# Two pairs of value groups merged into token-major groups of 1024 features, the linear attention's heads stepped evenly, the silu groups ended without a flush

## The chip, the core and the metric

The kernel runs on one core of a Trainium2 chip. The time is device microseconds of one execution. Matrix multiplications run on PE (TensorE), elementwise work on DVE (VectorE) and ACT (ScalarE); POOL (GpSimd) and SP (SyncE) here mostly issue transfers (DMAs). "mm" and "sm" are PSUM banks that PE writes, "u" and "ur" are buffers of 128x512 numbers in SBUF.

## The reference

One layer of a decoder trunk, 512 tokens of 1024 features in fp32. Of it, what the change touches:

```python
h = rmsnorm(x, ln1[i])
hq, hk, hv, hr, ha, hatt, hgate = _split_cols(h @ w_in[i], SPLIT_SIZES)
log_a = jax.nn.log_sigmoid((ha @ w_a2[i] + b_a[i]).astype(jnp.float32)) / GLA_TAU
o = gla_mixer(hq..., hk..., hv..., log_a...)              # 4 heads, dk 128, dv 256, chunks of 64 tokens
o = o * lax.rsqrt(jnp.mean(o * o, axis=-1, keepdims=True) + EPS)
o = o.reshape(B, S, GLA_V_W) * gla_gn[i] * jax.nn.silu(hr)
y_gla = o @ w_o_gla[i]
for g, (win, dil) in enumerate(((128, 1), (512, 4), (2048, 16))):
    o_g, lse_g = dilated_attention(q_g, k_g, v_g, bias_g, dil, win // dil)   # 4 heads of 128 each
wts = jax.nn.softmax(jnp.stack(lses, axis=0), axis=0)
o_att = jnp.sum(wts[..., None] * jnp.stack(outs, axis=0), axis=0)
y_att = o_att @ w_o_attn[i]
mix = (jax.nn.sigmoid(g_gla) * y_gla + jax.nn.sigmoid(g_att) * y_att) @ w_out[i]
```

Then an MLP of 4096, an embedding gate and a last norm, which the change leaves alone.

## The kernel before

Every fp32 product is emulated with three matmuls: each operand is split into a high part (`hi` for weights) and a low part (`lo`), and hi·hi, hi·lo and lo·hi are summed in PSUM. The input projection `h @ w_in` is cut into groups of 512 columns: the attention's q, k, v of its three groups (v1, v2 are the values of the two dilated ones, v0 those of the first), then gq, gk, gv0, gv1 of the linear attention (GLA), its output gate r0, r1, and the merge gates gb, ga. Most groups go through `strassen` (L301): a Strassen-Winograd scheme, in which seven products of half-size blocks take the place of eight. Each product is a stage (`STAGES`: A11, S1, A22, S2, A12, S4, S3), named after its weight block; S1 to S4 are sums of blocks A11 to A22. A stage is 24 matmuls of 128x256, all from one weight operand of 128x1024. A finished bank is evacuated by `begin` (to a buffer) or `end`, which adds it and calls the group's `finish`. Value groups are token-major: the tokens are the stationary side, the weights (`hi`, `lo`) stream.

The engines run in the order in which the program issues. `fetch` (L232) makes the weight operands, always at the same lead: in the turn of operand i it writes lo(i) on DVE (L239), hi(i+1) on ACT (L244), the sums S2 and S4 of operand i+2 on DVE (L218, L224), and prepares i+3: a load on SP's queue (L201), and for S1 and S3 an accumulating DMA on POOL's queue (L210, L221), which adds a second block from DRAM to the first. `EARLY` sets the lead of the load for S1: five operands before the group's A11. There are six buffers for loaded blocks, five for hi and four for lo, so that lo(i) waits until PE has used lo(i-4).

Other work runs between the matmuls. `run` (L255) issues pieces of eight matmuls and calls `step` (L179), which executes one entry of the list `later` (evacuations and what follows them) and, each `pace` streamed columns, one part of a generator in the list `side`. A yield is the end of a part. The generators are the scores and softmax of the attention (`scores0`, `scores12`), `weights` (the merge of the groups' softmax statistics), `pv`, `decay`, `gla(h)` (one head of the linear attention) and `gla_out`. `drain` issues whatever is left in both lists, `flush` whatever is left in `later`.

Three places matter below. `scores12` writes the softmax statistics of the dilated groups to DRAM (`s_dram`, L717), reads them back with tokens reordered (L719), and PE transposes them (L723); it runs beside v1 and v2. `values_cls` (L655) writes the finished values to DRAM (L662) and reads them back by residue class (L668). `gla(h)` needs one half of one gv group (L892 to L899 are its elementwise steps); heads 0 and 1 are started after gv0, heads 2 and 3 after gv1. `silu` multiplies r by its sigmoid: ACT L1060, DVE L1064.

Of the kernel before, what the change touches and what calls it, by code (L numbers as in the profile page):

```python
# [19 lines left out]
P = 128  # L20
T = 512
# [17 lines left out]
QUADS = ("quad", "quadt")  # L39
# [7 lines left out]
def weight_units():  # L47
# [14 lines left out]

    fm("k0", "w_in", att_col(0, 1), 4)
# [4 lines left out]
    quad("v1", "w_in", att_col(1, 2), "quadt")  # L68
    quad("v2", "w_in", att_col(2, 2), "quadt")
# [3 lines left out]
    quad("gv0", "w_in", GV, "quadt")  # L73
# [3 lines left out]
    quad("gv1", "w_in", GV + 512, "quadt")  # L77
# [48 lines left out]

# [3 lines left out]

EARLY = {max(i - LEAD, 0): n[:-4] for n, i in OPERAND.items() if n.endswith(".A11")}

# [15 lines left out]
def block_kernel(ctx, tc, xT, ws, pT, wts, wha, wa2, vec, lnf, rel, onehot, ident_d, mask_d, out):  # L148
# [55 lines left out]
    def prepare(i):  # L204

        name = OPERANDS[i]
        if i in EARLY:
            q = EARLY[i]
            w = raw[f"{q}.S1"] = load(f"{q}.A21")
            GP.dma_start(w, wts[UNIT[f"{q}.A22"]], accum_op=OP.add)  # L210
# [15 lines left out]
    def split_weights(tag, i, bufs):  # L226

        t = wsp.tile([P, 1024 + PAD], F32R, tag=tag, name=tag, bufs=bufs)
        o = SHIFT if OPERANDS[i] not in UNIT or UNITS[UNIT[OPERANDS[i]]][1] in QUADS else 0
# [25 lines left out]
    def run(mms, n=PIECE, shared=False):  # L255
        for i in range(0, len(mms), n):
            for o, l, r, a, b in mms[i:i + n]:
                TE.matmul(o, lhsT=l, rhs=r, start=a, stop=b, skip_group_check=shared)  # L258
            step(PIECE * r.shape[-1])
# [41 lines left out]
    def strassen(name, xo, finish, tm=False, scale=1.0, extra=None, acc=None):  # L301
# [36 lines left out]
        for i, s in enumerate(STAGES):  # L338
# [5 lines left out]
            if extra:  # L344
                extra(i)

# [163 lines left out]
    def xsums():  # L510
# [26 lines left out]
        yield from splits("T3", t3)  # L537

    def xs_op(name, pr):
        if name in ("B11", "B21", "B22"):  # L540
# [101 lines left out]
    def values(name, parts=False):  # L642
# [3 lines left out]
        def finish(m, t, s, ps):  # L646
            add(m, s, s, ps)
            res[m, t] = s
            if parts:
                split_later(s, res, (m, t))  # L650
# [3 lines left out]

    def values_cls(name):  # L655

        v_dram = dr.tile([T, 512], F32, name="v_dram")
        res, left = [], [4]

        def finish(m, t, s, ps):  # L660
            add(m, s, s, ps)
            GP.dma_start(v_dram[t * HT:(t + 1) * HT, m * HT:(m + 1) * HT].rearrange("(n p) c -> p n c", n=2),  # L662
                         s.rearrange("p (n c) -> p n c", n=2))
            left[0] -= 1
            if not left[0]:
                for c in range(4):
                    v = u32()
                    GP.dma_start(v, v_dram.rearrange("(m c) f -> c m f", c=4)[c])  # L668
                    res.append(v)

        strassen(name, xs_op, finish, tm=True)
# [23 lines left out]
    p12, p0 = [], []  # L695

    def scores12():
        for h in range(4):
# [7 lines left out]
            for cp in range(2):  # L706
# [3 lines left out]
                p12.append(pr)  # L710
        done12 = []
# [13 lines left out]
        V.tensor_copy(sn.rearrange("p a b -> p (a b)"), pst[:, 0:32])  # L725

# [16 lines left out]
    def weights():  # L743
# [3 lines left out]

        nmx, e0, e1, e2, dn, cn1 = (small(n) for n in ("nmx", "e0", "e1", "e2", "dn", "cn1"))
# [120 lines left out]
    def gla(h):  # L869
        b, q, k = gb_[h], gq[h], gk[h]  # L870
# [32 lines left out]
        vh = [cols(gv[h // 2][h % 2, p // 2], halves(p % 2)) for p in range(4)]  # L903
# [86 lines left out]
    def gla_out(h):  # L990
        for f in range(2):
            j = 2 * h + f
            pts = smt()
# [24 lines left out]
    q1 = qk_cls("q1", HD_SCALE)  # L1018
    side.append(scores0())
# [6 lines left out]
    v1 = values_cls("v1")  # L1026
    v2 = values_cls("v2")
    drain()
# [7 lines left out]
    gv = [values("gv0", True)]  # L1036
    drain()
    pace[0] = 4096
    side.extend(gla(h) for h in range(2))
# [5 lines left out]
    rg, tb, ga = [], [], []  # L1045

# [11 lines left out]
    def silu(js, outs, s, t):  # L1058
# [3 lines left out]
        def mult():  # L1062
            for n in range(2):
                V.tensor_tensor(outs[n], s[:, halves(n)], g[:, halves(n)], op=OP.mult)  # L1064
        later.append(mult)
# [504 lines left out]
```

## Time and profile before

| | |
|---|---|
| runs | 1033.85, 964.24, 963.78 us; median 964.24 |
| profiled execution | 964.0 us, of which the span of instructions is 962.2 |
| PE, DVE, ACT, POOL busy | 954.1, 743.2, 538.2, 103.6 us |
| moved | 138.92 MB, mean 144 GB/s |

The profile's page lists per engine the busy time, and per group of instructions (line, engine, operation, tiles) its count, busy time, mean duration in ns, and the idle time just before them with what ended it. The chain of waits is followed back from the last instruction. A timeline lists start, duration, engine, line, operation, tiles, and in brackets the idle time before it and what it waited for. Records of one engine overlap slightly, so what an instruction takes in a row of them is the distance from its start to the next one's.

### The profile page before, as it was taken

How to read it: one execution, taken by the hardware profiler on the slowest of the kernel's cores; microseconds unless marked ns; L12 is line 12 of the kernel's file. 1: busy time of each engine (PE TensorE's matmuls, PEld its weight loads, DVE VectorE, ACT ScalarE, POOL GpSimd, SP SyncE). 2: the span in 40 equal slices, each digit the busy share in tenths (PEclk: the TensorE clock that was granted, in tenths of full speed). 3: DMA queues.
4: the chain of work that ended last, by engine and by line, in shares of the span. 5: the costliest groups of instructions: out<-in, count | busy, mean ns of one | idle time of the engine just before them, and what ended most of it. 6: DMA issues, size and time to landing. Idle time of an engine off the chain costs nothing.

```text
span 962.2 us, 16747 instructions
## 1 busy us (share of the span) xinstructions
PE 954.1 (99%) x6734; PEld 894.2 (93%) x6734; DVE 743.2 (77%) x1064; ACT 538.2 (56%) x880; POOL 103.6 (11%) x145
## 2 busy tenths in 40 slices
PE   9999999999999999999999999999999999999997
PEld 8789999999998999999988899999998998988886
DVE  7688879676788769978856788777677899787754
ACT  7357547445657666675833446556665674354633
POOL 0140001420001021013010000011000100000000
PEclk9999999999999999999999999999999999999999
DMA  9385564964446555556536437565654464553102
GB/s 325 118 237 122 136 152 114 256 200 116 110 119 186 155 123 141 128 137 197 155 100 205 117 79 196 135 151 159 174 154 110 115 182 102 134 195 106 45 1 88
DMA packets 41326, 138.92 MB, mean 144 GB/s; under 512 B 5347, under 2 KB 5935, under 8 KB 41248
## 3 DMA queue, kind: packets, MB, share of 16 engines
q1 hardware_dynamic: 27648, 93.27, 29.2%
q0 software_dynamic: 12160, 42.20, 22.2%
q10 hardware_dynamic: 1440, 2.38, 0.7%
q8 instruction: 53, 0.87, 0.4%
q14 instruction: 25, 0.20, 0.1%
HBM read 131.50 MB, written 8.17 MB: 145 GB/s over the span
## 4 chain that ended last, share of the span: by engine, by line
PE 98%; DVE 1%; issue 1%; ACT 0%; POOL 0%; POOLq 0%; DVEq 0%; ACTq 0%
PE mmt L258 83%; PE smt L258 5%; PE mmt L480 2%; PE smt L867 1%; PE smt L807 1%; PE smt L732 1%; PE smt L452 0%; PE smt L824 0%; PE smt L705 0%; PE smt L813 0%; PE smt L704 0%; PE smt L823 0%; PE smt L995 0%; PE smt L1406 0%; PE smt L913 0%
## 5 line engine op out<-in xcount | busy, mean ns | idle before, releaser
L258 PE MATMUL mmt<-ur,hi 128*128 128x256 f32 (+1 forms) x3120 | 634.7, 301 | 0.0
L258 PEld LDWEIGHTS mmt<-ur,hi 128*128 128x128 f32 x3120 | 499.9, 188 | 21.6
L258 PE MATMUL mmt<-ur,lo 128*128 128x256 f32 (+1 forms) x1560 | 470.5, 302 | 0.0
L239 DVE TENSOR_TENSOR lo<-w,hi 128x1024 fp32r<-128x1024 f32 x250 | 303.1, 1219 | 50.3 <-PE mmt L258 32.4
L244 ACT ACTIVATE hi<-w 128x1024 fp32r<-128x1024 f32 x250 | 261.4, 1054 | 93.2 <-PE mmt L258 27.7
L258 PEld LDWEIGHTS mmt<-ur,lo 128*128 128x128 f32 x1560 | 293.8, 188 | 10.9
L258 PE MATMUL mmt<-hi,ur 128*128 128x256 f32 (+3 forms) x736 | 153.7, 306 | 0.0
L357 ACT ACTIVATE ur<-u 128x512 fp32r<-128x512 f32 x132 | 78.4, 624 | 104.4 <-DVE u L1107 30.9
L258 PEld LDWEIGHTS mmt<-hi,ur 128*128 128x128 f32 x736 | 118.5, 189 | 5.6
L350 DVE TENSOR_TENSOR u<-u,mmt 128x512 f32<-128x512 f32 (+1 forms) x124 | 78.3, 657 | 44.7 <-PE mmt L258 44.6
L258 PE MATMUL mmt<-lo,ur 128*128 128x256 f32 (+3 forms) x368 | 112.2, 305 | 0.0
L365 DVE TENSOR_TENSOR ur<-u,ur 128x512 fp32r<-128x512 f32 x131 | 86.3, 685 | 17.6 <-ACT ur L357 16.9
L332 ACT ACTIVATE u<-mmt 128x512 f32<-128x512 f32 x104 | 61.6, 592 | 55.8 <-PE mmt L258 55.5
L258 PEld LDWEIGHTS mmt<-lo,ur 128*128 128x128 f32 x368 | 69.4, 188 | 2.8
L221 POOL DMA_DIRECT2D w<-in_wts_dram x28 | 24.9, 888 | 360.6 <-DVE w L218 256.8
L210 POOL DMA_DIRECT2D w<-in_wts_dram x28 | 25.8, 920 | 273.1 <-DVE lo L239 66.0
L258 PE MATMUL smt<-ur,hi 128*128 128x512 f32 x160 | 50.4, 393 | 0.1
L258 PEld LDWEIGHTS smt<-ur,hi 128*128 128x128 f32 x160 | 29.8, 188 | 8.1 <-PE smt L562 0.8
L218 DVE TENSOR_TENSOR w<-w 128x1024 f32<-128x1024 f32 x28 | 34.3, 1225 | 1.0
L224 DVE TENSOR_TENSOR w<-w 128x1024 f32<-128x1024 f32 x28 | 34.3, 1225 | 1.0
L258 PE MATMUL smt<-ur,lo 128*128 128x512 f32 x80 | 31.2, 390 | 0.0
L390 ACT ACTIVATE u<-u 128x512 f32<-128x512 f32 x24 | 14.9, 622 | 16.7 <-DVE u L1188 16.7
(204 smaller groups left out, 714.5 us busy)
## 6 DMA issues: line engine op xcount, KB each, us to landing
w<-in_wts_dram SPq DMA_DIRECT2D x166, 512.0 KB, 4.4
w<-in_wts_dram POOLq DMA_DIRECT2D x56, 512.0 KB, 5.7
u<-in_xT_dram SPq DMA_DIRECT2D x8, 256.0 KB, 4.9
u<-in_ws_dram SPq DMA_DIRECT2D x8, 256.0 KB, 5.0
v_dram<-u POOLq DMA_DIRECT2D x8, 256.0 KB, 6.6
u<-v_dram POOLq DMA_DIRECT2D x8, 256.0 KB, 6.8
y_dram<-u ACTq DMA_DIRECT2D x8, 256.0 KB, 2.3
u<-y_dram POOLq DMA_DIRECT2D x8, 256.0 KB, 6.6
```

The costliest lines, as they stand in the source:

```text
L210: GP.dma_start(w, wts[UNIT[f"{q}.A22"]], accum_op=OP.add)
L218: V.tensor_tensor(w, w, raw[f"{q}.A11"], op=OP.add)
L221: GP.dma_start(w, wts[UNIT[f"{q}.A21"]], accum_op=OP.add)
L224: V.tensor_tensor(w, w, raw[f"{q}.A12"], op=OP.add)
L239: V.tensor_tensor(lo, w, hi.bitcast(F32), op=OP.subtract)
L244: S.activation(hi, w, AF.Copy)
L258: TE.matmul(o, lhsT=l, rhs=r, start=a, stop=b, skip_group_check=shared)
L332: S.activation(sums[c], bank[b], AF.Copy, scale=-scale if c[0] else scale)
L350: V.tensor_tensor(out, s, ps, op=OP.subtract if m else OP.add)
L357: S.activation(hi, x, AF.Copy)
L365: V.tensor_tensor(lo, x, hi.bitcast(F32), op=OP.subtract)
L480: TE.matmul(q0ps[i], lhsT=(hi, hi, lo)[j][:, c], rhs=(xh, xl, xh)[j], start=not k and not j, stop=k == KC - 1 and j == 2)
```

## The change

v1 and v2 become one group v12, gv0 and gv1 one group gv. Both go through the new function `wide`: the same seven products, with blocks twice as wide. A product has two weight operands (.0 and .1) and 24 matmuls of 128x512; the two token halves of a product go to two banks. The order of the products is `WIDE`: A11, S1, S2, A12, S3, S4, A22. S1 and S3 are loaded and accumulated (now L243 for all but the S3 of narrow groups, L258), S2 and S4 are summed on DVE (L252). The leads in `EARLY` become six operands ahead of a narrow group's S1, four for the S1 of the narrow group after a wide one, four for a wide S1, two for a wide S3.

In place of the drains after v2 and gv0 and ahead of the linear attention stand waits inside the generators: `weights` waits for the statistics (`sn_done`), `gla(h)` for all parts of gv, `gla_out` for the gates. All four heads of `gla` are appended ahead of gv and are stepped one after another by the pace, and one more yield stands after each head of `scores12`. The flushes after r0, gv1 and r1 go. The low parts of one activation block of the scheme (T3) are split in place into buffers of q1, once q1 is done.

```diff
+    def quadw(name, src, cs):
+
+        for m, k in ((0, 0), (1, 0), (1, 1), (0, 1)):
+            for i in range(2):
+                u.append((f"{name}.A{m + 1}{k + 1}.{i}", "quadw", src, 2 * i + k, cs[m]))
 
...
-    quad("v1", "w_in", att_col(1, 2), "quadt")
-    quad("v2", "w_in", att_col(2, 2), "quadt")
+    quadw("v12", "w_in", (att_col(1, 2), att_col(2, 2)))
...
-    quad("gv0", "w_in", GV, "quadt")
+    quadw("gv", "w_in", (GV, GV + 512))
...
-    quad("gv1", "w_in", GV + 512, "quadt")
...
-LEAD = 5
+WIDE = (("A11", "B11", "a"), ("S1", "T1", "c"), ("S2", "T2", "a"), ("A12", "B21", "b"), ("S3", "T3", "a"),
+        ("S4", "B22", "c"), ("A22", "T4", "a"))
+WBEGIN = {0: ((0, 0), "a"), 1: ((1, 1), "c"), 2: ((0, 1), "a")}
+WEND = {3: ((0, 0), "b"), 4: ((1, 1), "a"), 5: ((0, 1), "c"), 6: ((1, 0), "a")}
 
...
+        elif name.endswith("A11.0"):
+            names += [f"{name[:-5]}{a}.{i}" for a, _, _ in WIDE for i in range(2)]
...
-EARLY = {max(i - LEAD, 0): n[:-4] for n, i in OPERAND.items() if n.endswith(".A11")}
+EARLY = {}
+
+
+def early():
+    after_wide = False
+    for n, i in OPERAND.items():
+        q, _, what = n.partition(".")
+        if what == "S1":
+            EARLY.setdefault(max(i - (4 if after_wide else 6), 0), []).append((n, f"{q}.A21", f"{q}.A22"))
+            after_wide = False
+        elif what[:3] == "S1.":
+            EARLY.setdefault(i - 4, []).append((n, f"{q}.A21.{what[3:]}", f"{q}.A22.{what[3:]}"))
+            after_wide = True
+        elif what[:3] == "S3.":
+            EARLY.setdefault(i - 2, []).append((n, f"{q}.A11.{what[3:]}", f"{q}.A21.{what[3:]}"))
+
+
...
-        if i in EARLY:
-            q = EARLY[i]
-            w = raw[f"{q}.S1"] = load(f"{q}.A21")
-            GP.dma_start(w, wts[UNIT[f"{q}.A22"]], accum_op=OP.add)
+        for n, a, b in EARLY.get(i, ()):
+            w = raw[n] = load(a)
+            GP.dma_start(w, wts[UNIT[b]], accum_op=OP.add)
...
-        q, _, what = OPERANDS[i].rpartition(".")
-        if what == "S2":
+        q, _, what = OPERANDS[i].partition(".")
+        if what[:3] in ("S2.", "S4."):
+            a, b = ("S1", "A11") if what[1] == "2" else ("S2", "A12")
+            w = raw[OPERANDS[i]] = raw[f"{q}.{a}{what[2:]}"]
+            V.tensor_tensor(w, w, raw[f"{q}.{b}{what[2:]}"], op=OP.add)
+        elif what == "S2":
...
-            step(PIECE * r.shape[-1])
+            step(n * r.shape[-1])
...
+    def wide(name, xo, finish):
+
+
+        bank, sums = {}, {}
+
+        def begin(m, t, n, b):
+            def go():
+                sums[m, t, n] = u32()
+                S.activation(sums[m, t, n], bank[b][n], AF.Copy, scale=-1.0 if m else 1.0)
+            return go
+
+        def end(m, t, n, b):
+            return lambda: finish(m, t, n, sums.get((m, t, n)), bank[b][n])
+
+        for i, (op, xname, b) in enumerate(WIDE):
+            fresh = b not in bank
+            if fresh:
+                bank[b] = [smt() if b == "b" else mmt() for _ in range(2)]
+            for pr in range(4):
+                wh, wl = weight(f"{name}.{op}.{pr // 2}")
+                xh, xl = xo(xname, pr)
+                r = slice((pr % 2) * 512, (pr % 2 + 1) * 512)
+                mms = []
+                for n in range(2):
+                    c = slice(n * P, (n + 1) * P)
+                    for k, (l, w) in enumerate(((xh, wh), (xl, wh), (xh, wl))):
+                        mms.append((bank[b][n], l[:, c], w[:, r], fresh and not pr and not k, pr == 3 and k == 2))
+                run(mms, 3, shared=True)
+            if i in WBEGIN:
+                (m, t), b = WBEGIN[i]
+                later[0:0] = [begin(m, t, n, b) for n in range(2)]
+            if i in WEND:
+                (m, t), b = WEND[i]
+                later.extend(end(m, t, n, b) for n in range(2))
 
...
-        yield from splits("T3", t3)
+
+        while not q1_done:
+            yield
+        for g in range(2):
+            for p in range(2):
+                S.activation(xs[4 * g + 2 * p][0][:, halves(1)], t3[g][:, halves(p)], AF.Copy)
+        yield
+        for g in range(2):
+            for p in range(2):
+                hi, lo = cols(xs[4 * g + 2 * p], halves(1))
+                V.tensor_tensor(lo, t3[g][:, halves(p)], hi.bitcast(F32), op=OP.subtract)
+        yield
+
...
+    def whole(m, s, ps):
+
+        if s is None:
+            s = u32()
+            S.activation(s, ps, AF.Copy, scale=-1.0 if m else 1.0)
+        else:
+            add(m, s, s, ps)
+        return s
+
...
+            s, r = whole(m, s, ps), (2 * t + n) * P
+            GP.dma_start(v_dram[m][r:r + P, :], s)
...
+        while not sn_done:
+            yield
...
+        while len(gv) < 8:
+            yield
+        if h == 2:
+            for p in range(4):
+                split_later(gv[1, p], gv, (1, p))
+        while not all(isinstance(gv[h // 2, p], tuple) for p in range(4)):
+            yield
+        vh = [cols(gv[h // 2, p], halves(h % 2)) for p in range(4)]
...
+            while rg_done[j] < 2:
+                yield
...
-    v1 = values_cls("v1")
-    v2 = values_cls("v2")
-    drain()
+    v1, v2 = values_cls("v12")
...
-    gv = [values("gv0", True)]
-    drain()
-    pace[0] = 4096
-    side.extend(gla(h) for h in range(2))
+    gv = {}
+
+    def slower():
+        pace[0] = 4096
+        yield
+
+    side.append(slower())
+    side.extend(gla(h) for h in range(4))
+    values_parts("gv", gv)
+    pace[0] = 3072
...
-    flush()
+    pace[0] = 4096
     side.extend(gla_out(h) for h in range(2))
-    gv.append(values("gv1", True))
-    flush()
-    side.extend(gla(h) for h in range(2, 4))
     gates("r", 1, rg, silu)
-    flush()
     side.extend(gla_out(h) for h in range(2, 4))
```

The order of POOL's queue around the write of the statistics (`s_dram`). `w` is a weight block of 128x1024 that an accumulating DMA adds to; the last number ahead is that of v0.S1. Before:

```order
L221 DMA w_1428<-in_wts_dram 128x1024
L210 DMA w_1798<-in_wts_dram 128x1024
L717 DMA s_dram_1832<-st12_352 128x8x4
L719 DMA u_1834<-s_dram_1832 32x128
L662 DMA v_dram_1591<-u_1663 128x2x256
```

After (`w_1631` and `w_1669` are the two operands of v12.S3, `w_1796` is v0.S1):

```order
L243 DMA w_1631<-in_wts_dram 128x1024
L243 DMA w_1669<-in_wts_dram 128x1024
L243 DMA w_1796<-in_wts_dram 128x1024
L822 DMA s_dram_1815<-st12_352 128x8x4
L824 DMA u_1817<-s_dram_1815 32x128
L767 DMA v0_dram_1587<-u_1677 128x512
```

Three accumulations of a wide group's last products and of the next group now stand right ahead of the write, where one of v0.S1 and one of v2.S3 stood. On PE, the transposition of the statistics (the fourth row) stood between narrow products of v2; before:

```order
L258 MATMUL mmt<-hi,ur 128x256 x2
L258 MATMUL mmt<-lo,ur 128x256
L723 MATMUL smt<-ident,u 128x32
L258 MATMUL mmt<-hi,ur 128x256 x2
L258 MATMUL mmt<-lo,ur 128x256
```

After, it stands between two products of v12, at the first piece of S4.0:

```order
L295 MATMUL mmt<-hi,ur 128x512 x2
L295 MATMUL mmt<-lo,ur 128x512
L828 MATMUL smt<-ident,u 128x32
L295 MATMUL mmt<-hi,ur 128x512 x2
L295 MATMUL mmt<-lo,ur 128x512
```

From v12.S2.1 on, 60 matmuls of 128x512 stand ahead of it. On DVE, between lo(r1.S1) and lo(r1.A22) (the first and the last row; L350, now L422, adds a bank of PSUM to a buffer, L998 belongs to the norm of the linear attention's output); before:

```order
L239 TENSOR_TENSOR lo<-w,hi 128x1024
L218 TENSOR_TENSOR w<-w 128x1024
L350 TENSOR_TENSOR u<-u,mmt 128x512
L998 SCALAR_TENSOR_TENSOR u<-smt,cv,u 128x512
L365 TENSOR_TENSOR ur<-u,ur 128x512
L998 SCALAR_TENSOR_TENSOR u<-smt,cv,u 128x512
L350 TENSOR_TENSOR u<-u,mmt 128x512 x2
L365 TENSOR_TENSOR ur<-u,ur 128x512 x2
L239 TENSOR_TENSOR lo<-w,hi 128x1024
```

After (L985 to L1009 are the steps of `gla`, as L875 to L899 were; L1189 is the silu's product):

```order
L276 TENSOR_TENSOR lo<-w,hi 128x1024
L255 TENSOR_TENSOR w<-w 128x1024
L422 TENSOR_TENSOR u<-u,mmt 128x512
L992 COPY dec<-u 128x8
L993 TENSOR_TENSOR u<-u 128x512
L1189 TENSOR_TENSOR u<-u 128x256 x2
L1002 TENSOR_TENSOR u<-u 128x512
L1003 TENSOR_TENSOR u<-u 128x512
L1004 TENSOR_TENSOR u<-u,dec 128x4x64
L1005 COPY u<-u 128x4x64
L276 TENSOR_TENSOR lo<-w,hi 128x1024
```

The steps of two heads of `gla`, which stood in gb0, now stand among the lo splits of r1, with the products of silu.

More of the change, by code (lines that the diff above doesn't have):

```diff
@@ L228, in split_weights @@
         t = wsp.tile([P, 1024 + PAD], F32R, tag=tag, name=tag, bufs=bufs)
-        o = SHIFT if OPERANDS[i] not in UNIT or UNITS[UNIT[OPERANDS[i]]][1] in QUADS else 0
+        o = SHIFT if operand_kind(OPERANDS[i]) in ("quad", "quadt") else 0
         return t[:, o:o + 1024]
@@ L869, in gla @@
     def gla(h):
+        while len(gb_) <= h:
+            yield
         b, q, k = gb_[h], gq[h], gk[h]
@@ L1018, in block_kernel @@
     q1 = qk_cls("q1", HD_SCALE)
+    q1_done.append(True)
     side.append(scores0())
@@ L1045, in block_kernel @@
     rg, tb, ga = [], [], []
+    rg_done = [0] * KC
     def gates(name, i, res, make):
```

51 lines of the change are left out of this document (34 added, 17 removed).

## The prediction

> **What bounds the kernel now.** The profile's page comes first: engine totals, the granted clock, the shares of the chain of waits, the costliest groups, the DMA issues.
>
> ```profile
> PE 954.1 (99%) x6734; PEld 894.2 (93%) x6734; DVE 743.2 (77%) x1064; ACT 538.2 (56%) x880; POOL 103.6 (11%) x145
> ...
> PEclk9999999999999999999999999999999999999999
> ...
> PE 98%; DVE 1%; issue 1%; ACT 0%; POOL 0%; POOLq 0%; DVEq 0%; ACTq 0%
> ...
> L239 DVE TENSOR_TENSOR lo<-w,hi 128x1024 fp32r<-128x1024 f32 x250 | 303.1, 1219 | 50.3 <-PE mmt L258 32.4
> ...
> w<-in_wts_dram SPq DMA_DIRECT2D x166, 512.0 KB, 4.4
> w<-in_wts_dram POOLq DMA_DIRECT2D x56, 512.0 KB, 5.7
> ...
> v_dram<-u POOLq DMA_DIRECT2D x8, 256.0 KB, 6.6
> ```
>
> PE is busy 99% of a span of 962.2 us at full granted clock, and 98% of the chain is PE itself. No other engine's wait ends last for any length of time. So two things alone can move the time: what PE needs per column, and new holes in PE. Second view, the chain of waits in order of time; its columns are start, length, engine, tile, line and how many instructions the piece holds.
>
> ```profile
> 28.25 3.80 PE smt L258 x16
> ...
> 157.14 14.39 PE mmt L258 x120
> 171.71 22.03 PE mmt L258 x184
> 193.85 18.03 PE mmt L258 x152
> ...
> 912.08 36.33 PE mmt L258 x160
> ```
>
> The rows at 157, 171 and 193 are v1, v2 and v0, made of 128x256 matmuls: 14.39/120 = 119.9, 22.03/184 = 119.7, 18.03/152 = 118.6 ns each. The row at 912 is token-major work with 512 columns, both operands of the same kinds as the merged groups will have: 36.33/160 = 227.1 ns. The row at 28 has the same width with the weights as the stationary side: 3.80/16 = 237.5 ns.
>
> **Part 1, the merged width.** v1, v2, gv0 and gv1 hold 4 x 7 stages x 24 = 672 matmuls of 256 columns. In their place stand 2 x 7 x 24 = 336 operand products over 512 columns. Two narrow ones take 2 x 119.7 = 239.4 ns and a wide one 227.1, so 12.3 ns are saved 336 times: 4.1 us. If the wide ones cost what the row at 28 shows, 1.9 ns are saved, 0.6 us. I take 4.1, since the row at 912 has the same operands in the same roles; the ends are 0.6 and 4.3 (from 119.9 ns). The columns streamed and the multiplications are the same in number, so nothing else comes off PE. The Trainium skill, "TensorE: Matmul & The Clock Gate", section "Back-to-back issue gap", gives a warm gap of N/2.4 GHz plus 2.5 ns; an estimate from it is 109.2 and 215.8 ns, so a merged pair would save 2.5 ns and all of them 0.84 us. The rows here lie 10 to 12 ns above both its figures, which is where the larger saving comes from.
>
> **Part 2, the softmax statistics in the merged value group.** One matrix of statistics is written to DRAM, read back transposed, and turned on PE (L723 before, L828 after). The views are that line's own instructions, the DMA landings of its tile, the POOL timeline, and the landings of all weight tiles in 150 to 340 us.
>
> ```profile
> L723 PE MATMUL smt<-ident,u x1: 244/244/244, 171.5 to 171.5; 32*128 32x32 f32 x1
> ```
>
> ```profile
> DMA to landing us min/median/max: 3.2/3.6/3.9
> ```
>
> ```profile
> 149.07 0.86 POOL L210 DMA_DIRECT2D w<-in_wts_dram  x1 [8.33 <-DVE lo L239]
> 162.53 0.96 POOL L717 DMA_DIRECT2D s_dram<-st  x1 [12.60 <-DVE lo L239]
> 167.01 0.54 POOL L719 DMA_DIRECT2D u<-s_dram  x1 [3.53 <-issue]
> ...
> 198.00 2.19 POOL L668 DMA_DIRECT2D u<-v_dram  x4 [5.99 <-issue]
> 200.18 0.52 POOL L770 DMA_DIRECT2D k_dram<-u  x1
> 209.47 0.79 POOL L771 DMA_DIRECT2D cc<-k_dram  x1 [8.78 <-DMA k_dram<-u]
> ```
>
> ```profile
> DMA to landing us min/median/max: 3.3/5.4/10.0
> ```
>
> Before, the last accumulate ahead of the write was issued at 149.07, long done at 162.53. The read went out at 167.01 and takes 3.2 at the least: 170.2, against PE's use at 171.5. So 1.3 us were to spare. In the changed order the accumulate for v0.S1 stands on POOL directly ahead of the write. It is prepared in the turn of lo(v12.S3.0), whose buffer comes free only when PE begins v12.S2.1 (four lo buffers). From there: lo 1.2, the plain load 4.4 (the page), accumulate 5.7 if the write lands behind it, then 3.2 for the read and about 0.5 to issue: 15.0 us. That a small write lands behind larger ones on this queue is seen at 200.18: with four reads of 256 KB ahead, a write that otherwise lands in 3.6 was awaited until 209.47. The Trainium skill, "DMA: Bandwidth & Descriptors", section "SWDGE vs HWDGE vs iDMA", has only one such queue allocated; the 8.78 us agree. If it lands beside the accumulate, 0.9 + 3.6 stand for the 5.7: 13.8 us. PE has 60 wide matmuls from v12.S2.1 to the transposition: 60 x 227.1 ns = 13.6 us. So PE waits 0.2 to 1.4 us, and more where DVE is late with that lo: one w sum and one piece of softmax ahead of it, 1.2 + 1.4. The ends are 0.2 and 4.0; I take 2.5, near the upper half, since lo waits on its hi and both engines share this stretch with the softmax of four heads.
>
> **Part 3, the silu groups without a flush.** The flushes only emptied a list while PE had work queued: no hole in PE stands at them before, so they give back nothing. What is new is where DVE does the linear attention's heads 2 and 3. Before, they came as one pile at gb0; now their steps stand in r1, between its lo splits. Pitches from DVE's and ACT's timelines before, at that pile:
>
> ```profile
> 379.79 1.22 DVE L239 TENSOR_TENSOR lo<-w,hi 128x1024 fp32r<-128x1024 f32 x1
> 380.92 0.68 DVE L892 TENSOR_TENSOR u<-u 128x512 f32<-128x512 f32 x1
> 381.71 0.69 DVE L893 TENSOR_TENSOR u<-u 128x512 f32<-128x512 f32 x1
> 382.32 0.42 DVE L894 TENSOR_TENSOR u<-u,dec 128x256 f32<-128x256 f32 x1
> 382.65 0.29 DVE L895 COPY u<-u 128x256 f32<-128x256 f32 x1
> 382.85 1.22 DVE L239 TENSOR_TENSOR lo<-w,hi 128x1024 fp32r<-128x1024 f32 x1
> 383.99 0.68 DVE L350 TENSOR_TENSOR u<-u,mmt 128x512 f32<-128x512 f32 x1
> 384.59 0.28 DVE L897 COPY u<-u 128x256 f32<-128x256 f32 x1
> 384.79 0.41 DVE L898 TENSOR_TENSOR u<-u,dec 128x256 f32<-128x256 f32 x1
> 385.12 0.15 DVE L899 TENSOR_TENSOR dab<-dec 128x4 f32<-128x4 f32 x1
> 385.37 0.76 DVE L1064 TENSOR_TENSOR u<-u 128x256 f32<-128x256 f32 x2
> 386.04 0.29 DVE L897 COPY u<-u 128x256 f32<-128x256 f32 x1
> ...
> 393.95 2.35 DVE L239 TENSOR_TENSOR lo<-w,hi 128x1024 fp32r<-128x1024 f32 x2
> ```
>
> ```profile
> 380.53 1.28 ACT L1060 ACT_TABLE_LOAD   x1
> 384.70 0.63 ACT L1060 ACTIVATE u<-u 128x512 f32<-128x512 f32 x1 [2.89 <-DVE u L350]
> ```
>
> Start to start: lo or w sum 1.14; a 512 add 0.60; a 256 one 0.33; the block of L892 to L895 1.93; that of L897 to L899 0.78; two silu products 0.67. In the changed order DVE goes from the first output add of r0 (it waits for PE to end r0.A12) to lo(r1.A12) through six lo or w sums (5 x 1.14 + 1.22 = 6.9), four output adds (2.4), two q products (1.2), two 256 subtractions (0.66), two decay copies (0.3), three pairs of silu products (2.0), two blocks of 1.93 (3.9) and two of 0.78 (1.6): 18.9 us. PE has six stages in that time: 6 x 24 x 119.7 ns = 17.2. So lo is 1.7 late and PE waits for it. On top come DVE's waits for ACT: the silu products wait for a sigmoid, and ACT's order has three table loads among r1's first stages (sigmoid, exp, sigmoid) at 1.28. None or all of them may show: 1.7 to 1.7 + 3.8 = 5.5. I take 3.5, half of it. Before, the same pile at gb0 left lo(gb0.A22), the first of the two at 393.95, just in time for PE, without a hole; nothing there says that more fits.
>
> **Parts at nothing.** The drains after the value groups and ahead of the linear attention: PE has no hole there before. The wide group's split of T3 in place: its ACT copies and DVE subtractions lie a group ahead of their use. The value groups' way through DRAM: the accumulate for v0.S3, v0's last stage, now stands on POOL behind four reads of v12's first half. From the end of v12.S4 PE has 24 wide matmuls of A22 and six stages of v0, 5.4 + 17.2 = 22.6 us; the stores take 6.6, four reads and something small behind them 9.3 (200.18 to 209.47), an accumulate in its place 5.7 - 3.6 = 2.1 more, lo 1.2 and as much for hi: 20.4. Loads: a wide group reads ten plain and four accumulated pieces of 512 KB, 7.3 MB in 14 x 12 x 0.2271 = 38.2 us, 192 GB/s. DVE in gv: 11 lo and 4 w sums (17.1) and about 15.2 of adds, splits and head steps, 32.3 us, against 11 operands x 12 x 0.2271 = 30.0 of PE; the 2.3 over are covered by the lead of up to two operands (5.4) that four lo buffers give, and cost 2.3 if DVE comes into gv late.
>
> **Sum.** 964.0 (the profiled run: span 962.2 and 1.8 around it; the median of the runs is 964.24) - 4.1 + 2.5 + 3.5 = 965.9 us. The forecast's own ends: 964.0 - 4.3 + 0.2 + 1.7 = 961.6 and 964.0 - 4.1 + 4.0 + 5.5 = 969.4.
>
> **Rivals.** (a) The gain stays and neither operand is late: 964.0 - 4.1 = 959.9. For it: PE hid every pile of DVE work before, and each of the two waits is a small difference between long sums. Against: both sums come out positive. 0.25. (b) The width gives little: 964.0 - 0.6 + 2.5 + 3.5 = 969.4. For it is the row at 28, against it the row at 912. By the skill's gap rule, cited above, it would be 969.2. 0.10. (c) DVE is late through gv too, and the waits at their upper ends: 964.0 - 4.1 + 4.0 + 5.5 + 2.3 = 971.7. 0.08. (d) Slower: the wide groups starve for weights. The queue of SP already waits for buffers:
>
> ```profile
> SPq L201 <- DVE lo L239: 782.3, 152, 19.1
> ```
>
> That is 782.3 us in 152 waits: a load starts only when a lo has freed a buffer. From its issue to its hi lie two operand turns, 2 x 12 x 227.1 ns = 5.45 us; the page's load lands in 4.4, but the longest landing above is 10.0. Each load that is so late opens a hole of 4.55 us. Six of the twenty plain loads of the two groups: 959.9 + 6 x 4.55 = 987.2. It decides from a landing above 5.45. Against it: narrow groups have as many bytes per PE time and open no hole. 0.04. That the width isn't what PE runs is no rival: the changed order has 128x512 matmuls in those groups.
>
> **How the numbers follow.** Forecast 0.53, the rivals 0.25, 0.10, 0.08, 0.04. Range 959.5 to 970.5: it holds the forecast's ends, (a) and (b), and leaves out (c), (d) and a little beside them. A measurement of this kernel tells about 2% from no change, 19.3 us: under 945.0 or over 983.5. Faster needs 19 us off PE, where the change can give 4.3: 0.01. Slower is (d): 0.04. Within: 0.95.
>
> **What would show it.** The chain's pieces in v12 and gv: 227 ns a matmul (237 is rival b). PE idle ahead of the transposition at L828, with the statistics' write on POOL right after an accumulate of L243. PE idle at L295 ahead of r1's A22, S2 or A12, put down to DVE's lo of L276. Elsewhere no hole above a microsecond. No hole at both places is rival (a); holes at wide operands, put down to DMA, are (d). I am wrong if PE's busy time falls by more than 4.5 us, or if it waits somewhere that isn't named here.

## The result and the profile after

The changed kernel took 974.62 us in the median of five runs (974.06 to 974.79), the kernel before 964.34. The ratio is 1.0106, with a 95% interval of 1.0092 to 1.0121: 1.1% slower. (The 1033.85 us in the table of the kernel before is an execution in a slower state and stays out of the ratio.) The profiled execution took 974.8 us, its span is 973.0.

The page of the changed kernel: engine totals, granted clock by slices, shares of the chain, and the accumulating loads (median from issue to landing).

```profile
PE 954.4 (98%) x6398; PEld 879.1 (90%) x6398; DVE 741.0 (76%) x1062; ACT 539.1 (55%) x882; POOL 99.4 (10%) x145
...
PEclk9999999899999999999999999999999999999999
...
PE 87%; DVE 5%; ACT 3%; issue 2%; DMA 2%; POOL 0%; POOLq 0%; DVEq 0%; ACTq 0%
...
w<-in_wts_dram POOLq DMA_DIRECT2D x56, 512.0 KB, 5.9
```

PE has 336 matmuls fewer and is not less busy: its busy time gained about as much elsewhere as the width took off. The chain, which was PE for 98%, is PE for 87%. The granted clock has one slice of 8. The chain of waits of the changed kernel shows where (start, length, engine, tile, line, count):

```profile
165.20 5.44 PE smt L295 x24
170.64 5.45 PE mmt L295 x24
176.09 6.54 issue
182.92 12.40 PE mmt L295 x45
```

The wide matmuls cost what was expected, 5.45/24 = 227.1 ns. Then PE stands still for 6.5 us. It is the wait at the transposition of the statistics (L828, a row of PE's timeline), and behind it the clock is halved for 4 us (a row of the windows: stretch, its length, busy times of PE, its weight loads, DVE, ACT, POOL, then granted clock, DMA share, GB/s):

```profile
182.64 0.28 PE L828 MATMUL smt<-ident,u 32*128 32x32 f32 x1 [6.56 <-issue]
```

```profile
183.00:187.00 4.00, 4.00 (x10) 3.13 (x11) 1.28 (x2) 0.00 (x0) 1.37 (x2) 0.50 0.94 251
```

From the transposition's start at 182.64 to 187.20 PE does it and ten matmuls in 4.56 us. At 227 ns each, and 0.17 for the transposition as in the kernel before, it would be 2.44, so 2.1 us are lost there at half the clock. This also keeps PE's busy time up. POOL's timeline for the same place:

```profile
169.43 0.87 POOL L243 DMA_DIRECT2D w<-in_wts_dram  x1 [18.18 <-DMA w<-in_wts_dram]
169.97 1.28 POOL L822 DMA_DIRECT2D s_dram<-st  x1
180.71 0.55 POOL L824 DMA_DIRECT2D u<-s_dram  x1 [9.46 <-DMA s_dram<-st]
181.25 2.18 POOL L767 DMA_DIRECT2D v_dram<-u  x4
```

The write of the statistics is issued half a microsecond behind the accumulation for v0.S1, and the read waits for it until 180.71; in the kernel before, 4.5 us lay from write to read (162.53 to 167.01). Just ahead of it SP sends five loads of weights within 5 us, each as soon as one of DVE's five instructions from 164.03 to 169.8 (three lo splits and two sums, back to back) has freed a buffer. SP's timeline and two rows of DVE's:

```profile
165.28 4.87 SPq L235 DMA_DIRECT2D w<-in_wts_dram  x5
```

```profile
164.03 1.22 DVE L276 TENSOR_TENSOR lo<-w,hi 128x1024 fp32r<-128x1024 f32 x1
...
168.57 1.22 DVE L276 TENSOR_TENSOR lo<-w,hi 128x1024 fp32r<-128x1024 f32 x1
```

The second place is r1: three holes, all put down to the lo split on DVE, on which the silu's products (L1189) wait for ACT, which loads function tables. PE's timeline, DVE's and ACT's:

```profile
377.66 0.38 PE L295 MATMUL mmt<-ur,lo 128*128 128x256 f32 x1 [1.55 <-DVE lo L276]
...
381.86 0.39 PE L295 MATMUL mmt<-ur,lo 128*128 128x256 f32 x1 [1.00 <-DVE lo L276]
386.14 0.39 PE L295 MATMUL mmt<-ur,lo 128*128 128x256 f32 x1 [1.18 <-DVE lo L276]
```

```profile
364.52 0.69 DVE L422 TENSOR_TENSOR u<-u,mmt 128x512 f32<-128x512 f32 x1 [1.38 <-PE mmt L295]
...
367.06 0.76 DVE L1189 TENSOR_TENSOR u<-u 128x256 f32<-128x256 f32 x2 [1.18 <-ACT u L1185]
...
373.84 0.76 DVE L1189 TENSOR_TENSOR u<-u 128x256 f32<-128x256 f32 x2 [1.67 <-ACT u L1185]
...
384.87 1.22 DVE L276 TENSOR_TENSOR lo<-w,hi 128x1024 fp32r<-128x1024 f32 x1
```

```profile
365.10 1.28 ACT L1185 ACT_TABLE_LOAD   x1
...
367.05 1.28 ACT L995 ACT_TABLE_LOAD   x1
...
371.88 1.28 ACT L1185 ACT_TABLE_LOAD   x1
```

From the first add of r0 (364.52) to the end of lo(r1.A12) (386.09) DVE needs 21.6 us, of which 1.18 + 1.67 = 2.85 are waits for ACT.

The account: the width gives -4.3 (a run below), the hole at the transposition +6.7, the halved clock behind it +2.1, the three holes in r1 +1.7 + 1.2 + 1.3 = 4.2 (measured from start to start of the matmuls, less what a matmul takes), two holes of 0.3 and 0.4 at 227 and 311 us +0.7. That is +9.4 of the 10.8 between the two profiled spans; 1.4 us lie in gaps too small to be assigned.

### The profile page after: what moved, and what is told of

Its sections match the earlier page's. It is cut to its first block, busy times and chain, and to the rows that moved or that the text cites. A ratio compares the mean times of both kernels' runs of the same rounds, so it can differ in the third digit from the quotient of the medians.

```text
span 973.0 us, 16072 instructions
## 1 busy us (share of the span) xinstructions
PE 954.4 (98%) x6398; PEld 879.1 (90%) x6398; DVE 741.0 (76%) x1062; ACT 539.1 (55%) x882; POOL 99.4 (10%) x145
## 4 chain that ended last, share of the span: by engine, by line
PE 87%; DVE 5%; ACT 3%; issue 2%; DMA 2%; POOL 0%; POOLq 0%; DVEq 0%; ACTq 0%
PE mmt L295 73%; PE smt L295 5%; PE mmt L552 2%; DVE lo L276 2%; PE smt L975 1%; DMA v_dram<-u 1%; DVE ur L437 1%; PE smt L838 1%; ACT hi L281 1%; DMA k_dram<-u 1%; PE smt L915 0%; PE smt L524 0%; DMA cc<-k_dram 0%; ACT ur L429 0%; DVE u L422 0%
## 5 line engine op out<-in xcount | busy, mean ns | idle before, releaser
L295 PEld LDWEIGHTS mmt<-ur,hi 128*128 128x128 f32 x3120 | 499.7, 188 | 21.6
L295 PE MATMUL mmt<-hi,ur 128*128 128x512 f32 (+3 forms) x480 | 133.9, 365 | 0.2 <-DVE u L422 0.2
L422 DVE TENSOR_TENSOR u<-u,mmt 128x512 f32<-128x512 f32 (+1 forms) x116 | 73.1, 656 | 35.4 <-PE mmt L295 35.3
L295 PEld LDWEIGHTS mmt<-hi,ur 128*128 128x128 f32 x480 | 86.1, 190 | 13.4 <-issue 0.6
L295 PE MATMUL mmt<-lo,ur 128*128 128x512 f32 (+3 forms) x240 | 86.9, 362 | 0.0
L369 ACT ACTIVATE u<-mmt 128x512 f32<-128x512 f32 x88 | 52.2, 594 | 53.0 <-PE mmt L295 52.7
L243 POOL DMA_DIRECT2D w<-in_wts_dram x32 | 29.4, 961 | 306.0 <-DMA w<-in_wts_dram 113.9
L258 POOL DMA_DIRECT2D w<-in_wts_dram x24 | 21.2, 884 | 339.0 <-DVE w L255 223.9
L295 PEld LDWEIGHTS mmt<-lo,ur 128*128 128x128 f32 x240 | 45.5, 190 | 6.7
L255 DVE TENSOR_TENSOR w<-w 128x1024 f32<-128x1024 f32 x24 | 29.4, 1225 | 0.8
L261 DVE TENSOR_TENSOR w<-w 128x1024 f32<-128x1024 f32 x24 | 29.4, 1225 | 0.8
```

The costliest lines, as they stand in the source:

```text
L243: GP.dma_start(w, wts[UNIT[b]], accum_op=OP.add)
L255: V.tensor_tensor(w, w, raw[f"{q}.A11"], op=OP.add)
L258: GP.dma_start(w, wts[UNIT[f"{q}.A21"]], accum_op=OP.add)
L261: V.tensor_tensor(w, w, raw[f"{q}.A12"], op=OP.add)
L369: S.activation(sums[c], bank[b], AF.Copy, scale=-scale if c[0] else scale)
L422: V.tensor_tensor(out, s, ps, op=OP.subtract if m else OP.add)
```

## The experiments

All edits are to the changed kernel unless another is named. The kernel before was run with each set: 963.96 to 964.29 us in the median. Where a hole is given without a row, it is the distance between two starts of matmuls on PE, less the duration of one.

**1. The transposition later.**

```diff
-        for _ in range(6):
+        for _ in range(12):
             yield
         pst = smt()
```

> The changed kernel, with the transposition of the statistics on PE twelve parts after the write in place of six; each part is six wide matmuls, so PE reaches it 6 x 1.36 = 8.2 us later. POOL's queue stays as it is. Theory (the hole at the transposition is a wait of its own): the hole of 6.7 us goes, and with it the eight matmuls at 427 in place of 227 ns behind it (1.6 to 2.0 us): 974.6 - 8.5 = 966.1 us, granted clock 1.0 in that stretch. Rival (the transfers are late altogether, so PE only waits somewhere later, at v0.S1 or at the merge of the statistics): 970 or more, with a new hole within 25 us behind the old one.

Measured: 972.89 us, 1.0092 of the kernel before (1.0075 to 1.0109). The rival is right. The hole at the transposition is gone, but 24 us later PE has one of 4.5 us, with 2.1 us lost to the clock behind it. A row of PE's timeline of this run, of ACT's, and two of POOL's:

```profile
208.46 0.80 PE L295 MATMUL mmt<-hi,ur 128*128 128x256 f32 x2 [4.35 <-ACT u L369]
```

```profile
205.43 1.06 ACT L281 ACTIVATE hi<-w 128x1024 fp32r<-128x1024 f32 x1 [12.08 <-DMA w<-in_wts_dram]
```

```profile
192.39 2.13 POOL L772 DMA_DIRECT2D u<-v_dram  x4 [8.93 <-issue]
194.51 0.95 POOL L258 DMA_DIRECT2D w<-in_wts_dram  x1
```

The load that PE waits for is the accumulation for v0.S3. It is issued at 194.51, behind the four reads of the value groups, and lands 10.8 us later. The reads wait for stores, the stores were queued behind the read of the statistics. ACT is held by its hi for it, and the copy out of PSUM (L369) that frees PE's bank stands behind that hi. So the late write delayed all that follows on POOL's queue; the hole at the transposition only covered it. Run 2, where the write is early, gives the size: the same accumulation lands at 201.9 in place of 205.4 us, and PE's hole behind it is 0.6 in place of 4.5.

**2. The accumulation behind the write.**

```diff
-            EARLY.setdefault(max(i - (4 if after_wide else 6), 0), []).append(...)
+            EARLY.setdefault(max(i - (3 if after_wide else 6), 0), []).append(...)
```

> The changed kernel, with the accumulation for v0.S1 one operand later, so that on POOL it stands behind the write and the read of the statistics. Theory (the small write lands behind the accumulation that was issued ahead of it): the write lands in 3 to 5 us in place of 10.2, no hole at the transposition, 966 us. Rival (the write is slow because five loads of SP share the transfer engines with it): it still takes 8 us or more, a hole of 2 us or more stays, 968 to 970 us.

Measured: 967.29 us, 1.0034 (1.0023 to 1.0045): 7.3 us of the 10.3 come back by one operand's lead. (The edit also moves the accumulation for r0.S1, behind gv, by one operand; PE has no new hole there.) POOL's timeline of this run, and SP's:

```profile
164.96 0.96 POOL L822 DMA_DIRECT2D s_dram<-st  x1 [14.45 <-DVE lo L276]
171.08 0.54 POOL L824 DMA_DIRECT2D u<-s_dram  x1 [5.16 <-issue]
171.62 0.95 POOL L243 DMA_DIRECT2D w<-in_wts_dram  x1
```

```profile
164.69 4.87 SPq L235 DMA_DIRECT2D w<-in_wts_dram  x5
```

The write is issued 5.0 us earlier, since it no longer stands behind an instruction that waits for a load, and lands in 5.6 us in place of 10.2. So with the accumulation out of its way the write is fast enough. How the 4.6 us divide is not shown: SP sends the same five loads, but the write now goes out behind the first of them, where in the changed kernel all five were ahead of it. Above the 3.9 us of the kernel before, where one load was in flight, 1.7 us are left, and the loads are the likely cause. The Trainium skill, "DMA: Bandwidth & Descriptors", section "Issuing engines are not separate DMA queues", says that transfers started by different engines run on the same transfer engines and interleave; the 1.7 us agree in direction. A hole of 0.7 us stays at the transposition, and 0.6 and 1.1 us at v0.S3 and behind it.

**3. The heads back to gb0.**

```diff
-    side.extend(gla(h) for h in range(4))
+    side.extend(gla(h) for h in range(2))
     values_parts("gv", gv)
...
     gates("r", 1, rg, silu)
+    side.extend(gla(h) for h in range(2, 4))
     side.extend(gla_out(h) for h in range(2, 4))
```

> The changed kernel, with heads 2 and 3 of the linear attention appended behind r1, so that their steps on DVE stand in gb0, as in the kernel before, and no longer in r1. Theory (the three holes in r1, 1.7 + 1.2 + 1.3 us, are DVE's extra work there and its waits for ACT): they go, 974.6 - 4.2 = 970.4 us. Rival (the work only moves, and DVE is as late in gb0): the holes stand in gb0, 973 to 975 us.

Measured: 982.46 us, 1.0188 (1.0173 to 1.0203), slower than anything expected. The holes in r1 are gone. New ones stand in gb0 and behind it as DVE works off the heads later: 0.8 at 405, 2.2 + 1.3 + 1.0 at 447 to 454, and 3.5 at 490, where the projection behind the linear attention waits for a split of its input, with the clock halved behind it. Two rows of PE's timeline:

```profile
449.15 0.50 PE L295 MATMUL mmt<-ur,hi 128*128 128x256 f32 x2 [2.05 <-ACT u L369]
...
493.79 1.52 PE L295 MATMUL mmt<-ur,hi 128*128 128x512 f32 x2 [3.31 <-ACT ur L429]
```

So the work has to lie somewhere between gv and the output projection, and r1 is not its worst place. Nor did the kernel before have it in gb0, as the opening section, the prediction and the expectation of this run say. Counted on PE, its r1 lasts from 365.5 to 385.8 us, and its DVE does the steps of heads 2 and 3 from 372.5 to 386.7: in r1, but for the last microsecond. Most of the silu's products of r1 follow in gb0. What is new in r1 are the last output adds of r0 and its silu products, done by 346.8 us before, with gv1 still to come, and with them ACT's changes between silu's table and that of the heads. The run therefore tries a third place, and does not go back to the first.

**4. No table loads in r1.** Silu's sigmoid is replaced by an exponential, so the gate has other values; the number of instructions on DVE is the same.

```diff
-        S.activation(g, s, AF.Sigmoid)
+        S.activation(g, s, AF.Exp)
```

> The changed kernel, with silu's sigmoid computed as an exponential: a part of the computation is changed, ACT no longer switches its function tables among r1's first stages; DVE's work is the same. Theory (of the 4.2 us in r1, DVE's own work makes 1.7 and its two waits for ACT the rest): the holes shrink to 1.0 to 2.2 us in sum, 972.0 to 973.0 us there, and no other hole changes. Rival (DVE's own work alone makes PE wait): 974.6 us.

Measured: 971.35 us, 3.3 us less than the changed kernel. Of the three holes, the one at A22 goes, the one at S2 shrinks to 0.3, the one at A12 stays at 1.3: 1.6 in place of 4.2 us in r1. One row of PE's timeline is left there:

```profile
383.59 0.39 PE L295 MATMUL mmt<-ur,lo 128*128 128x256 f32 x1 [1.18 <-DVE lo L276]
```

DVE's own work makes 1.6 us of the lateness, its waits for ACT's tables 2.6. DVE's stretch from the first add of r0 to the end of lo(r1.A12) takes 18.8 us here (364.76 to 383.53), in place of 21.6. The 0.7 us beyond that are the shorter hole at the transposition in this execution (6.3 in place of 6.7) and what lies between executions.

**5. The heads earlier, on run 2's kernel.**

```diff
     values_parts("gv", gv)
-    pace[0] = 3072
+    pace[0] = 2048
```

> The kernel of the run with the later accumulation for v0.S1, and beside it the pace behind gv set to 2048 columns in place of 3072, so that the steps of heads 2 and 3 of the linear attention are issued in r0.S4, r0.S3 and r1.A11, ahead of most silu products of r1. Theory (the holes in r1 are a pile of two heads' steps, silu's products and table loads in one place): the three holes of 4.2 us go but for at most 1 us, 967.3 - 4.2 = 963.1 us, up to 964. Rival (DVE has no room for the heads anywhere near r0 and r1, so the holes come earlier): 966 to 968 us, holes in r0.

Measured: 965.32 us, 1.0012 (1.0003 to 1.0021), 2.0 less than run 2. The holes of 4.2 us in r1 become one of 1.9, at the bank that ACT has to copy out:

```profile
377.32 0.51 PE L295 MATMUL mmt<-ur,hi 128*128 128x256 f32 x2 [1.74 <-ACT u L369]
```

The copy is late since ACT's hi ahead of it waits for r1.S3's accumulation (2.4 us in the profile of run 6, which has the same hole), and that accumulation is issued only behind the late lo of r1.S1 and its sum. And the hole of 1.1 at the probabilities is 1.5 in this execution, so the gain is 2.0 and not 4.2. The time lies between the theory's and the rival's.

**6. The reads behind, on run 5's kernel.**

```diff
-            if not left[m]:
-                for c in range(4):
...
+            if not any(left):
+                for m in range(2):
+                    for c in range(4):
```

> The kernel before it in this call, with all eight reads of the value groups from DRAM issued when both groups are written, so that on POOL the accumulation for v0.S3 stands ahead of the reads and not behind four of them. Theory (the accumulation landed 9 to 11 us after its issue because four reads were ahead of it on a queue that lands in order): it lands in 6 us or less, the holes of 0.6 and 1.1 us at v0.S3 and behind it go, 963.1 - 1.5 = 961.6 us. Rival (the statistics that come back behind eight reads make PE wait at the probabilities instead): 963 us or more with a hole behind 210 us.

Measured: 963.45 us, 0.9995 (0.9986 to 1.0004), 1.9 less than run 5. POOL's timeline:

```profile
186.50 0.92 POOL L258 DMA_DIRECT2D w<-in_wts_dram  x1 [2.60 <-DMA w<-in_wts_dram]
188.03 1.23 POOL L767 DMA_DIRECT2D v_dram<-u  x2 [0.60 <-ACT e L862]
189.76 2.13 POOL L773 DMA_DIRECT2D u<-v_dram  x4 [0.51 <-issue]
```

The accumulation for v0.S3 lands in 7.1 us, at 193.6, where it landed at 202.0 in run 2. The holes at v0.S3 and at the probabilities are gone, as the theory has it, though 7.1 us is more than its 6; its 961.6 us started from a run 5 that was expected at 963.1. Left are 0.9 at the transposition, 1.9 in r1 and 0.4 at 302.

**7. The width alone, on run 6's kernel.** Each wide matmul is issued as two of 256 columns.

```diff
                     for k, (l, w) in enumerate(((xh, wh), (xl, wh), (xh, wl))):
-                        mms.append((bank[b][n], l[:, c], w[:, r], ...))
-                run(mms, 3, shared=True)
+                        for z in range(2):
+                            mms.append((bank[b][n][:, halves(z)], l[:, c], w[:, r][:, halves(z)], ...))
+                run(mms, 6, shared=True)
```

> The kernel before it in this call, with each matmul of 512 columns of the two merged groups issued as two of 256, in the same order, into the same banks, with the same work between: only the width differs. Theory (a matmul costs 12 ns beyond its columns): 336 x 12.3 ns = 4.1 us longer than that kernel. Rival (the wide ones cost what the narrow ones do but for 2 ns a pair): 0.6 to 0.9 us longer.

Measured: 966.11 us, 2.7 more than run 6. The price per product is seen in the chain, first of run 6, then of this run, the same two stages of v12:

```profile
164.81 5.44 PE smt L295 x24
170.25 5.45 PE mmt L295 x24
```

```profile
165.87 5.76 PE smt L295 x48
171.63 5.76 PE mmt L295 x48
```

5.45 against 5.76 us: 12.9 ns a pair, 336 x 12.9 = 4.3 us. Of these, 1.6 came back at once: the slower stream has no hole at the transposition and 1.2 in place of 1.9 in r1. A faster PE arrives earlier at operands whose time is set by other engines. By the gap rule of the Trainium skill that the prediction cites it would be 0.84 us; the measurement decides against it for these operands.

**8. The flushes put back, on run 6's kernel.**

```diff
     gates("r", 0, rg, silu)
+    flush()
...
     gates("r", 1, rg, silu)
+    flush()
```

> The kernel with the reads behind, with the flushes after r0 and r1 put back. Theory (a flush only empties a list while PE has work queued): within 0.5 us of that kernel, no new hole. Rival (issuing the evacuations and silu's products of a group's end at once makes the next lo late): a hole of 1 us or more at r1.A11 or gb0.A11.

Measured: 968.54 us, 1.0045 (1.0031 to 1.0058), 5.1 more than run 6. The rival is right but for the place, r1.A22 in place of r1.A11 or gb0.A11. The silu's products are issued in one pile and the lo behind them is late:

```profile
371.58 0.39 PE L295 MATMUL mmt<-ur,lo 128*128 128x256 f32 x1 [2.21 <-DVE lo L276]
```

Behind this hole the clock is at 0.59 from 372 to 376, and two further holes of 1.3 and 0.7 us stand at 453 and 457 us. In run 6's kernel, with its order of the heads, ending without a flush is worth 5 us.

**9 and 10. Run 6's kernel with the transposition two parts later; and with another pace.**

```diff
-        for _ in range(6):
+        for _ in range(8):
...
     values_parts("gv", gv)
-    pace[0] = 2048
+    pace[0] = 2560
```

Run 9 has the first of these edits, run 10 both.

> The kernel with the reads behind, and the transposition of the statistics eight parts after the write in place of six (2.7 us later on PE). Theory (the hole of 0.9 us left there is only the read's landing): it goes, the one of 1.9 us in r1 stays, 963.4 - 0.9 = 962.5 us. Rival (the time comes back at v0 or at the probabilities, as in the run with twelve parts): 963.4 us, a hole behind 200 us.

> The same with the pace behind gv at 2560 columns in place of 2048, so that the steps of heads 2 and 3 lie one or two operands later, in r0.S3 to r1.S1. Theory (the hole of 1.9 us is lo(r1.S1) being late behind both heads' steps, its sum and its accumulation with it): with the steps spread over one operand more it shrinks to under 1 us, 961.5 us. Rival (later means into silu's products and table loads, as in the changed kernel): 2 to 4 us of holes in r1, 963.5 to 965 us.

Measured: 963.07 us, 0.9992 (0.9983 to 1.0001), and 963.04 us, 0.9991 (0.9982 to 1.0000). In both the hole at the transposition is gone and none comes in v0. The hole in r1 stays, 2.1 us in run 9 and 2.0 in run 10, where it moves from a bank at A12 to the lo split at A22. Run 9's profile is of the slowest of its 11 executions, 965.38 us. A row of run 10:

```profile
368.99 0.39 PE L295 MATMUL mmt<-ur,lo 128*128 128x256 f32 x1 [1.82 <-DVE lo L276]
```

So in these three runs the pace only chose where the two heads are late. These are the best versions found. They lie 1.0 us below the kernel before, with intervals that reach 1.0: no more than level with it. The 4.3 us of the width are not all in hand as long as this hole stays; with all holes gone it would be 964.0 - 4.3 = 959.7, which no run reached.

**11. The transposition nine parts after the write.** As run 1, with 9 in place of 12.

> The changed kernel with the transposition nine parts after the write in place of six: PE reaches it 4.1 us later and waits there 6.7 - 4.1 = 2.6 us. Theory on the clock (the slow phase follows a hole of more than 2.3 us): matmuls of 512 columns at about 430 ns for some 3 to 4 us behind it, and a second hole at v0.S3 as in the run with twelve parts, smaller by the time PE lost here. Rival (a hole has to be longer than 3.4 us): 227 ns right behind the hole.

Measured: 968.62 us from two executions (967.40, which is the profiled one, and 969.83), 1.0047 (1.0029 to 1.0066). PE waits 3.35 us at the transposition, a little more than expected, and no hole follows at v0.S3. The clock does not fall behind it: matmuls at 227 ns (PE's timeline), granted clock 1.00 from 182.8 to 188.

```profile
182.78 0.22 PE L828 MATMUL smt<-ident,u 32*128 32x32 f32 x1 [3.19 <-issue]
182.92 0.73 PE L295 MATMUL mmt<-hi,ur 128*128 128x512 f32 x2
183.49 0.39 PE L295 MATMUL mmt<-lo,ur 128*128 128x512 f32 x1
183.72 0.62 PE L295 MATMUL mmt<-hi,ur 128*128 128x512 f32 x2
```

The threshold of 2.3 us is wrong, and so is any threshold on the hole alone (below).

## Why the prediction was wrong

The forecast was 965.9 us, with a range of 959.5 to 970.5; it came to 974.6. Both places of new holes were named, and PE has no other hole above a microsecond. The step that failed is the size of the second part.

- *Part 1, the width: -4.1.* Right. Run 7 gives 4.3 us. Rival (b) is out.
- *Part 2, the statistics: +2.5, ends 0.2 and 4.0.* This is the term that was mis-sized: it is 6.7, with 2.1 behind it at half the clock, 8.8 us in all. The mechanism is the one described (run 2). Link by link, in the profile of the changed kernel: from PE's start on v12.S2.1 (162.3) to the end of lo(v12.S3.0) 2.9 us, between the 1.2 and 3.8 given; the load 3.6, for which 4.4 was taken; 0.6 until POOL issues; the accumulation and the write behind it 11.3 (169.43 to 180.71), where the sum had 5.7 and 0.5; the read 1.8, where it had 3.2. So one link carries the miss. 5.7 was the page's median over the whole kernel, taken for a moment in which SP sends five loads within 5 us; this accumulation by itself landed in 9.4 us (169.43 to 178.86), the one at 150.39, with one load of SP beside it, 5.4. That the loads make the difference is argued from the trace; no run took them away. They come in one burst because DVE, late behind the softmax, frees five buffers back to back. A row that would have warned stood in the prediction, the longest landing of 10.0 us; it was used only for a rival. The profile before had a nearer one, the DMA issues of 168 to 190 us, where three accumulations landed in 7.3 us in the median:

```profile
w<-in_wts_dram POOLq DMA_DIRECT2D x3, 512.0 KB, 7.3
```

- *The halved clock.* No term stood for it. Behind the hole of 6.7 us it cost 2.1. Whether the forecast's 2.5 us would have paid it can't be said: holes of 2.4 and 2.1 us did in runs 8 and 9, one of 3.35 us in run 11 did not.
- *Part 3, the heads in r1: +3.5, ends 1.7 and 5.5.* Right: 4.2 us in r1, of which 1.6 is DVE's own work (run 4; the sum gave 1.7) and 2.6 its waits for the table loads. DVE's stretch is 21.6 us in the profile against 18.9 + 2.85, and 18.8 without the loads (run 4). Wrong is what it says of the kernel before: the heads' pile stood in r1 there too, without r0's silu (run 3).
- *The flushes at nothing.* Right of the kernel before, where PE had no hole at them. In the new order they are not free: the two put back into run 6's kernel cost 5.1 us (run 8). The removal is no part of the loss as far as that run shows; in the changed kernel itself it was not tried.
- *The reads ahead of v0.S3's accumulation at nothing.* Wrong as a matter of cover: 20.4 of 22.6 us was a margin of 2.2, and the late write used it up. In the changed kernel the hole at the transposition hides that; run 1 shows 4.5 us there, run 2 leaves 0.6, and run 6 removes that.
- *DVE in gv at nothing.* Right: its chain passes through DVE from 287 to 311 us, with a hole of 0.4 and no more.
- Of the rivals, (a) and (d) did not happen. (c) came nearest in size, 971.7, but by other places.

## What to carry to other kernels

Cost a transfer by the landings at its own moment, with what else is in flight there and what stands ahead of it on its queue, not by its median over the kernel; a chain of several such transfers through one queue is as late as its worst link makes it, and what queues behind it is late as well. When PE has no holes, every saving on PE shortens the time that hides the other engines: before counting it, list the operands whose lead is below what is saved plus a few microseconds. And a removed wait has to be followed to the next thing on the same queue, as run 1 did: the wait that was seen hid another.

## What the runs showed of the hardware

A hole on PE can cost its own length and 2 to 3 us more. Behind holes of 3.5 us (run 3), 4.5 (run 1) and 6.3 to 6.7 us (the changed kernel, runs 3 and 4), matmuls take twice their time for 4 to 6 us. The length alone does not decide it. Behind 3.35 us in run 11, and behind 1.9 and 2.0 us in runs 6 and 10, the clock stayed at 1.00. Behind 2.4 us in run 8 and 2.1 us in run 9 it fell (granted clock 0.59 from 372 to 376 us and 0.66 from 375 to 380).

The granted clock of these traces changes only on a grid of 3.41 us, which lies at another place in each execution. In the changed kernel it changes at 6.18, 180.26 and 187.09 us, in run 8 at 4.09, 372.73 and 379.55, in run 9 at 7.04, 375.68 and 379.09: 51, 108 and 108 steps of 3.413 us, then 2, 2 and 1. Windows of two stretches on the grid each, of the changed kernel, of run 9 and of run 11 (the first figure behind the length is PE's busy time, the figure behind POOL's the clock):

```profile
176.85:180.26 3.41, 0.00 (x0) 0.00 (x0) 0.00 (x0) 0.15 (x1) 0.00 (x0) 1.00 0.97 335
180.26:187.09 6.83, 4.45 (x11) 3.55 (x12) 1.32 (x2) 0.00 (x0) 3.65 (x6) 0.50 0.68 192
```

```profile
372.27:375.68 3.41, 1.48 (x13) 1.24 (x12) 3.31 (x5) 2.01 (x4) 0.86 (x1) 1.00 0.84 180
375.68:379.09 3.41, 3.41 (x19) 3.41 (x17) 2.69 (x6) 3.41 (x7) 0.00 (x0) 0.50 0.94 238
```

```profile
177.99:181.41 3.42, 1.60 (x8) 0.98 (x6) 0.00 (x0) 1.06 (x1) 1.31 (x3) 1.00 1.03 329
181.41:184.82 3.41, 2.04 (x9) 1.75 (x10) 1.79 (x3) 0.45 (x1) 2.33 (x4) 1.00 0.90 315
```

Behind a step with PE busy for 0.00 or 1.48 us (1.21 in run 8, 1.26 in run 1) the clock is halved; behind the steps with 1.60 and 2.04 us, over which run 11's hole is spread, it is not. So in these traces it counts how much of a hole falls into one step. This holds for every step at full clock ahead of the last 15 us of each kernel; there the clock also fell behind steps with PE idle for only 0.7 to 1.0 us (runs 7, 10 and 11), so idle time is not all that counts. The Trainium skill, "TensorE: Matmul & The Clock Gate", section "What's actually happening", describes a window of about 3.4 us that runs on its own and halves the clock after an idle one. The grid and its free place agree; that 1.9 of 3.4 us idle were enough does not fit the need of a whole idle window, and the measurement decides. One kernel can therefore go either way: run 11's other execution took 969.83 us at a mean granted clock of 0.994, the profiled one 967.40 at 0.997.
